# Modulation sections with four column sets side by side and one sum per section; gate rows broadcast by DMA through DRAM

## The chip, the cores and the metric

The kernel runs on one core of one Trainium2 chip. The metric is the device time of one execution in microseconds (us). Inside the core TensorE (PE; its weight loads are PEld), VectorE (DVE), ScalarE (ACT) and GpSimd (POOL) each work through their own instructions in order; SyncE (SP) issues all DMA transfers of this kernel, in order too.

## What is computed

Two layers of an encoder over 256 tokens of width 1024. Each layer has a token mixer (attention, retention and a state space branch S5) and a convolutional feed-forward net (FFN). What matters here is the modulation by the vector c:

```python
cond = jax.nn.silu(c)
for l in range(DEPTH):                       # DEPTH = 2
    mod = cond @ w_ada[l] + b_ada[l]         # (1, 1024) @ (1024, 6144)
    shift1, scale1, gate1, shift2, scale2, gate2 = jnp.split(mod, 6, axis=-1)
    h = layer_norm(x) * (1.0 + scale1) + shift1
    merged = ...                             # the mixer, fed by h @ w_in[l]
    x = post_norm(ALPHA * x + gate1 * (merged @ w_o[l]))
    h = layer_norm(x) * (1.0 + scale2) + shift2
    x = post_norm(ALPHA * x + gate2 * conv_ffn(h))
```

So there are twelve modulation sections of 1024 values, six in a layer, and each is a product of one row with a 1024x1024 matrix. A shift or a scale is needed as a column (the channel lies on the partitions); a gate is needed as a row that stands in all 128 partitions.

## The kernel before, in words

Tokens lie in two tiles of 128 (t = 0 and 1). Weights come from DRAM as loads of 128x1024 floats (512 KB), named `raw` for the main weights and `ada` or `adab` for `w_ada`. The main weights are split into two parts (`hi` by ACT, `lo` by DVE), so that a product takes three matmuls; some products (`g_ps`) use `raw` itself.

**The modulation** is done by `ada_chunk` (L1110). A section is four chunks of 256 columns, a chunk is two loads, and a load holds four row blocks of 128 times 256 columns. Four matmuls with 32-column weights (`condz`, in which only the first of 32 columns is not zero) write the four row blocks' partial sums side by side into partitions 0, 32, 64 and 96 of one PSUM bank, `ada_ps`; the second load adds to them. Then ACT copies the bank to `z`. For a gate, a matmul with a 128x128 matrix of ones (L1126) adds the four partial sums and puts the result into all partitions, and DVE adds the bias row (`rows`, L1128). For a shift or scale, two transposes (L1131) bring `z` to columns, DVE adds the four (L1133) and then the bias.

**The order.** All operations are recorded first. A planner (`Recorder.schedule`, L546) then sets each engine's order, from costs, priorities in recorded order, and free buffers. Six kinds of place matter:
- `need` (L1153) inserts chunks between weight loads of the mixer (`spread`, L1890). The rest (`adab`) are recorded behind the boundaries (L1896, L1908).
- A **boundary** (`boundary`, L1264) follows the mixer and the FFN. For t = 0 and then t = 1, DVE multiplies the result by the gate (`y`), normalizes (`bst`, `bmv`, `ve`, `x`) and prepares the next norm; POOL gives `rstd`. The normalized `xn` is transposed on PE (`h_ps`), modulated by ACT (`hf`), split (`hh`, `hlo`), and feeds the next product (`upt` for the FFN, `b_` for the next mixer).
- Before the first boundary of a layer stand the output product `wo_acc` and, ahead of it, `br_ps`, which waits for `th` and `osl` (DVE) behind `glu_ps`.
- The S5 branch sends a matrix `R` through DRAM (`rd`, L1740) and loads it back as 32 transfers named `T`, which PE needs for `Y`.
- SP issues in the planned order; an issue waits until its tile is free and its source is there.
- `rot` (L1331) makes rotation tables of the next layer on DVE, wherever the planner finds room.

Of the kernel before, what the change touches and what calls it, by code (L numbers as in the profile page):

```python
# [10 lines left out]
F32 = mybir.dt.float32  # L11
# [3 lines left out]
ALU = mybir.AluOpType  # L15
AX = mybir.AxisListType
# [3 lines left out]
D = 1024  # L20
S = 256
P = 128
# [36 lines left out]
SEC = ("shift1", "scale1", "gate1", "shift2", "scale2", "gate2")  # L59


def _rows(w):
    k = w.shape[0] // P
    return w.reshape(k, P, w.shape[1]).transpose(1, 0, 2)
# [82 lines left out]
    return out  # L147


def _ada(w, l, key):  # L150
    c, k = (int(v) for v in key[3:].split("_"))
    return _rows(w["w_ada"][l][k * 512:(k + 1) * 512, c * 256:(c + 1) * 256]).reshape(P, -1)


# [32 lines left out]
def _host(w):  # L187
# [3 lines left out]
    for g in _stream():  # L191
        cols = [(_ada(w, l, key) if fn is None else fn(w, l)).astype(f32, copy=False)
                for l, key, width, fn in g]
        parts.append(np.concatenate(cols, axis=1).ravel())
# [537 lines left out]
def build(tc, A, dbg=None):  # L732
    nc = tc.nc
    ctx = ExitStack()
    rec = Recorder()

    def pool(name, bufs, **kw):
        return Pool(rec, ctx.enter_context(tc.tile_pool(name=name, bufs=1, **kw)), bufs, kw.get("space") == PSUM)

    cp = pool("const", 1)  # L740
    drp = pool("dram", 1, space=DRAM)
# [6 lines left out]
    V, G, T, AC, SY = (Engine(rec, n, e) for n, e in (  # L748
        ("DVE", nc.vector), ("POOL", nc.gpsimd), ("PE", nc.tensor), ("ACT", nc.scalar), ("SP", nc.sync)))
    mm = T.matmul  # L750

    def t4(shape, name, dt=F32):
        return k4.tile(shape, dt, tag="k4", name=name)
# [4 lines left out]
    def t1(shape, name, dt=F32):  # L758
        return k1.tile(shape, dt, tag="k1", name=name)

    def bank(shape, name):
        return psp.tile(shape, F32, tag="ps", name=name)
# [10 lines left out]
    def tt(out, a, b, op, eng=None, flex=False):  # L773

        eng = eng or main[0]
        eng.tensor_tensor(out=out, in0=a, in1=b, op=op, **({"alt": G if eng is V else V} if flex else {}))

    def ts(out, a, s1, op0, s2=None, op1=None, eng=None):
        eng = eng or main[0]
        if eng is G and op1 is None:  # L780
            s2, op1 = 1.0, ALU.mult
        kw = {} if op1 is None else {"op1": op1}
        eng.tensor_scalar(out=out, in0=a, scalar1=s1, scalar2=s2, op0=op0, **kw)

    def stt(out, a, s, op0, b, op1):
        if main[0] is V:
            V.scalar_tensor_tensor(out=out, in0=a, scalar=s, in1=b, op0=op0, op1=op1)
        else:
            tmp = gtmp[:, 0:a.shape[1]]
            ts(tmp, a, s, op0)  # L790
            tt(out, tmp, b, op1)
# [14 lines left out]
    for gi, g in enumerate(groups):  # L806
        offs.append(o)
        c = 0
# [6 lines left out]
    def raw_chunk(l, key, tile_=None):  # L815

        gi, c, width = where[l, key]
        if gi not in loaded:
            w = sum(x[2] for x in groups[gi])
            t = loaded[gi] = tile_ or t4([P, 1024], "raw")  # L820
            SY.dma_start(out=t[:, 0:w], in_=A["wts"][offs[gi]:offs[gi] + P * w].rearrange("(p w) -> p w", p=P))
        return loaded[gi][:, c:c + width]
# [33 lines left out]
    ident = const[:, 0:P]  # L856
    dist = const[:, P:640]

    def sm(name, a=0, b=None):
        lo, hi = off[name]  # L860
        return small[:, lo + a:(hi if b is None else lo + b)]

    ones = cp.tile([P, P], F32, name="ones")
    V.memset(ones, 1.0)
    mhalf = cp.tile([P, 16], F32, name="mhalf")
    gtmp = cp.tile([P, 80], F32, name="gtmp")
    G.memset(mhalf, -0.5)
# [6 lines left out]
    condz = cp.tile([P, 8, 32], F32, name="condz")  # L874
# [223 lines left out]
    modc = {}  # L1098
    gate_rows = {}

    def row_tile(l, i):
        t = t4([P, D], "rows" if i < 2 else "lnrow")
        SY.dma_start(out=t, in_=A["rows"][l, i:i + 1, :].to_broadcast([P, D]))
        return t

    for l in range(L):
        for s in ("shift1", "scale1", "shift2", "scale2"):
            modc[l, s] = cp.tile([P, 8], F32, name=f"mod{l}{s}")

    def ada_chunk(l, c, kind=None):  # L1110
        sec, sub = SEC[c // 4], c % 4
        ps = bank([P, 512], "ada_ps")
        for j in range(2):
            raw = t4([P, 1024], kind or "ada")
            raw = raw_chunk(l, f"ada{c}_{j}", raw).rearrange("p (k n) -> p k n", k=4)
            with rec.group():
                for k in range(4):
                    mm(out=ps[32 * k:32 * k + 32, 0:256], lhsT=condz[:, 4 * j + k], rhs=raw[:, k],
                       start=(j == 0), stop=(j == 1))
        z = t1([P, 256], "z")  # L1120
        AC.copy(z, ps[:, 0:256])
        if sec.startswith("gate"):
            i = 0 if sec == "gate1" else 1
            if sub == 0:
                gate_rows[l, sec] = row_tile(l, i)
            mm(out=ps[:, 256:512], lhsT=ones, rhs=z, start=True, stop=True)  # L1126
            g = gate_rows[l, sec][:, sub * 256:(sub + 1) * 256]
            tt(g, ps[:, 256:512], g, ALU.add)  # L1128
        else:
            for b in range(2):  # L1130
                T.transpose(ps[:, 256 + b * P:256 + (b + 1) * P], z[:, b * P:(b + 1) * P], ident)  # L1131
            m = modc[l, sec][:, 2 * sub:2 * sub + 2]
            V.tensor_reduce(out=m, in_=ps[:, 256:512].rearrange("p (b c d) -> p b c d", b=2, d=32)[:, :, :, 0],  # L1133
                            op=ALU.add, axis=AX.X)
            ib = ("shift1", "scale1", "shift2", "scale2").index(sec)
            bcol = sm("b_ada", l * 32 + ib * 8 + 2 * sub, l * 32 + ib * 8 + 2 * sub + 2)
            if sec.startswith("scale"):
                stt(m, m, 1.0, ALU.add, bcol, ALU.add)
            else:
                tt(m, m, bcol, ALU.add)  # L1140


    pending, pace = [], [0, 1]
# [5 lines left out]
    def settle():  # L1149
        while pending:  # L1150
            ada_chunk(*pending.pop(0))

    def need(l, key):  # L1153
        pace[0] += 1
        if pending and pace[0] > 0 and pace[0] % pace[1] == 0:
            rec.bias = ADA_BIAS
            ada_chunk(*pending.pop(0))
            rec.bias = 0
        return chunk(l, key)
# [222 lines left out]
    def mixer(l, xt, h, s5, xdram, ready=None, pre_=None):  # L1382
# [10 lines left out]
        if h is None:  # L1393
            h, xn = new_h(l, 1), [norm(x) for x in xt]
            for k in range(0, 8, 2):
                for c in (k // 2, 4 + k // 2):
                    ada_chunk(l, c, "ada0")
                for t in range(2):
                    put_h(h, l, 1, t, xn[t], [k, k + 1])
                gemm_t(need(l, f"b0_{k}"), h, 416, k, o0, k == 0, k == 6)  # L1400
                b1(k)
            rope_tables()
            rec.bias = PRE_BIAS
            prephase()
            s5.prep()
            s5.rot()
            rec.bias = 0
        elif ready is not None:
            ps0, ps1 = ready[0:2], ready[2:4]
            o0 = [q[:, 0:416] for q in ps0]  # L1410
# [476 lines left out]
    h, s5, start = None, S5(0), None  # L1887
    for l in range(L):
# [12 lines left out]
        if more:  # L1901
            start = Start(l + 1, FIRST)
# [37 lines left out]
```

## Time and profile before

| | us |
|---|---|
| three runs, median | 1078.13 (1076.7 to 1079.13) |
| the profiled execution, its own time | 1076.2 |
| its span | 1074.3 |
| PE busy | 998.9 (93%) |
| DVE busy | 860.2 (80%) |
| ACT busy | 492.0 (46%) |

The profile names the line of the recording helper (L728) for nearly all instructions, so they are told apart by tile. The stages in the order of time: first norm and modulation (0 to 130), first mixer (130 to 345), first boundary (345 to 375), FFN (to 553), second boundary (553 to 600), second mixer (to 857), its boundary (857 to 890), FFN and last norm. All DMA goes through SP: 212 MB in all.

### The profile page before, as it was taken

Reading aid. Unit: us, or ns where it says so; the run is one execution under the profiler, and the core shown is the slowest. Engines: PE = TensorE matmul, PEld = TensorE weight load, DVE = VectorE, ACT = ScalarE, POOL = GpSimd, SP = SyncE. Lnnn points to the kernel's source line nnn. Section 1 sums busy time; section 2 is a strip of 40 time slices with the busy share of each in tenths; the row PEclk is TensorE's granted clock in tenths of the full one; section 3 lists DMA queues with packets and bytes.
Section 4 is the critical chain, followed back from the end, with each engine's and each line's share of the span. In section 5 each row is a group of like instructions: output and inputs, shape, how many; then the busy total and the mean of one; then the engine's idle time right before and its main releaser. Section 6 shows DMA issues by size and latency. Waiting matters only on the chain.

```text
span 1074.3 us, 20654 instructions
## 1 busy us (share of the span) xinstructions
PE 998.9 (93%) x8148; PEld 852.6 (79%) x8148; DVE 860.2 (80%) x1783; ACT 492.0 (46%) x888; POOL 37.8 (4%) x43
## 2 busy tenths in 40 slices
PE   4878999998999999999989999998699979999996
PEld 2557876776888689999967988777599859999995
DVE  7999999973569998777888997997365698777775
ACT  2353343212563666555635645411256456555640
POOL 0010000000001100000011000000000010000001
PEclk9989999998999999999998999999899989999998
DMA  8963235448874966555559532543877437555510
GB/s 337 408 231 125 92 125 190 155 121 268 326 261 168 377 244 222 190 179 178 169 197 374 187 117 77 219 157 79 259 252 274 138 120 233 187 189 193 200 36 40
DMA packets 66849, 212.09 MB, mean 197 GB/s; under 512 B 7744, under 2 KB 16064, under 8 KB 66752
## 3 DMA queue, kind: packets, MB, share of 16 engines
q1 hardware_dynamic: 66752, 210.77, 56.2%
q8 instruction: 64, 1.05, 0.4%
q14 instruction: 33, 0.27, 0.1%
HBM read 207.66 MB, written 3.08 MB: 196 GB/s over the span
## 4 chain that ended last, share of the span: by engine, by line
PE 66%; DVE 10%; DMA 3%; ACT 1%; issue 1%; POOLq 0%; SPq 0%; DVEq 0%; ACTq 0%
PE up_ps L728 22%; PE dn_acc L728 11%; PE g_ps L728 10%; PE br_ps L728 4%; PE ada_ps L728 3%; PE wo_acc L728 2%; PE upt L728 2%; PE b L728 2%; DVE g L728 2%; DMA ada<-in_wts 1%; DVE w L728 1%; DVE y L728 1%; PE u_ps L728 1%; PE glu_ps L728 1%; DVE x L728 1%
## 5 line engine op out<-in xcount | busy, mean ns | idle before, releaser
L728 DVE TENSOR_TENSOR lo<-raw,hi 128x1024 fp32r<-128x1024 f32 (+1 forms) x210 | 251.3, 1214 | 65.1 <-PE up_ps L728 20.1
L728 ACT CAST hi<-raw 128x1024 fp32r<-128x1024 f32 (+1 forms) x210 | 214.3, 1043 | 73.2 <-DVE lo L728 18.3
L728 PE MATMUL up_ps<-hh,lo 128*128 128x256 f32 x640 | 181.1, 283 | 0.0
L728 PE MATMUL up_ps<-hlo,hi 128*128 128x256 f32 x640 | 181.1, 283 | 0.0
L728 PE MATMUL up_ps<-hh,hi 128*128 128x256 f32 x640 | 181.0, 283 | 0.0
L728 PE MATMUL g_ps<-hw,raw 128*128 128x256 f32 x512 | 124.8, 387 | 0.0
L728 PEld LDWEIGHTS up_ps<-hh,hi 128*128 128x128 f32 x640 | 122.7, 192 | 1.7 <-DVE g L728 0.4
L728 PEld LDWEIGHTS up_ps<-hlo,hi 128*128 128x128 f32 x640 | 122.7, 192 | 1.2
L728 PEld LDWEIGHTS up_ps<-hh,lo 128*128 128x128 f32 x640 | 122.7, 192 | 0.1
L728 PEld LDWEIGHTS g_ps<-hw,raw 128*128 128x128 f32 x512 | 94.2, 192 | 16.8 <-issue 5.8
L728 DVE SCALAR_TENSOR_TENSOR cv<-up_ps,small,cv 128x255 f32<-128x255 f32 x176 | 73.2, 475 | 13.0 <-ACT cv L728 12.8
L728 PE MATMUL dn_acc<-lo,ah 128*128 128x512 f32 x176 | 68.7, 391 | 0.0
L728 PE MATMUL dn_acc<-hi,al 128*128 128x512 f32 x176 | 67.1, 390 | 0.0
L728 PE MATMUL dn_acc<-hi,ah 128*128 128x512 f32 x176 | 66.8, 392 | 0.0
L728 ACT ACTIVATE cv<-up_ps,small 128x256 f32<-128x256 f32 x88 | 44.9, 562 | 33.4 <-PE up_ps L728 33.0
L728 ACT ACTIVATE gt<-g_ps 128x256 f32<-128x256 f32 x48 | 18.4, 384 | 86.2 <-PE g_ps L728 86.1
L728 ACT CAST hl<-raw 128x512 fp32r<-128x512 f32 x48 | 28.9, 619 | 42.6 <-DMA raw<-in_wts 19.1
L728 DVE TENSOR_TENSOR hl<-raw,hl 128x512 fp32r<-128x512 f32 x48 | 32.5, 685 | 16.4 <-ACT hl L728 16.1
L728 DVE TENSOR_TENSOR w<-g,g 128x512 f32<-128x512 f32 x64 | 42.9, 685 | 0.7 <-PE br_ps L728 0.5
L728 POOL TENSOR_TENSOR rstd<-ve,mhalf 128x1 f32<-128x1 f32 (+1 forms) x28 | 30.0, 1077 | 347.7 <-DVE ve L728 347.7
L728 DVE TENSOR_TENSOR g<-bC,pw 128x512 f32<-128x512 f32 x64 | 41.7, 682 | 0.1
L728 DVE TENSOR_TENSOR g<-pw,bbt 128x512 f32<-128x512 f32 x64 | 41.0, 684 | 0.0
(324 smaller groups left out, 2149.6 us busy)
## 6 DMA issues: line engine op xcount, KB each, us to landing
raw<-in_wts SPq DMA_DIRECT2D x262, 512.0 KB, 4.4
ada<-in_wts SPq DMA_DIRECT2D x48, 512.0 KB, 9.5
adab<-in_wts SPq DMA_DIRECT2D x48, 512.0 KB, 7.0
T<-rd SPq DMA_DIRECT2D x64, 64.0 KB, 3.1
lnrow<-in_rows SPq DMA_DIRECT2D x8, 512.0 KB, 5.2
raw<-in_wts SPq DMA_DIRECT2D x8, 416.0 KB, 6.9
x<-in_x SPq DMA_DIRECT2D x4, 512.0 KB, 7.2
rows<-in_rows SPq DMA_DIRECT2D x4, 512.0 KB, 6.5
```

Source lines behind the costliest of these rows:

```text
L728: getattr(o.eng.real, method)(*a, **kw)
```

## The change

The sections shift1 and scale1 of layer 0 stay as they were. For the other ten, `ada_part` replaces the sum by chunk:
- A load now holds one row block of 128 with all 1024 columns of the section. Its four matmuls share the weights of that row block, and their outputs side by side are four sets of 256 columns instead of four partial sums. All eight loads of a section add to the same bank.
- After the last load, and only then, one copy to `z` and, for shift and scale, two transposes and one addition with the bias.
- For a gate, the four rows of `z` are written to DRAM by four DMAs (`zd`, 1 KB each), one DMA reads them back into all 128 partitions (512 KB, `rows<-zd`), and one DVE addition of 128x1024 adds the bias row, which is loaded as before. The matrix of ones is gone.

```diff
+def ada_rows(l, c):
+    return (l, c // 4) not in ((0, 0), (0, 1))
 def _ada(w, l, key):
     c, k = (int(v) for v in key[3:].split("_"))
+    if ada_rows(l, c):
+        k += 2 * (c % 4)
+        return w["w_ada"][l][k * P:(k + 1) * P, c // 4 * D:(c // 4 + 1) * D]
...
-    ones = cp.tile([P, P], F32, name="ones")
-    V.memset(ones, 1.0)
...
+    def ada_part(l, c, kind):
+        sec, sub = SEC[c // 4], c % 4
+        if sub == 0:
+            ada_bank[l, sec] = bank([P, 512], "ada_ps")
+        ps = ada_bank[l, sec]
+        for j in range(2):
+            raw = t4([P, 1024], kind or "ada")
+            raw = raw_chunk(l, f"ada{c}_{j}", raw)
+            with rec.group():
+                for q in range(4):
+                    mm(out=ps[32 * q:32 * q + 32, 0:256], lhsT=condz[:, 2 * sub + j], rhs=raw[:, q * 256:(q + 1) * 256],
+                       start=(sub + j == 0), stop=(sub == 3 and j == 1))
+        if sub < 3:
+            return
+        z = t1([P, 256], "z")
+        AC.copy(z, ps[:, 0:256])
+        if sec.startswith("gate"):
+            i = 0 if sec == "gate1" else 1
+            brow, g = row_tile(l, i), t4([P, D], "rows")
+            zd = drp.tile([1, D], F32, name=f"zd{l}{i}")
+            for q in range(4):
+                SY.dma_start(out=zd[:, q * 256:(q + 1) * 256], in_=z[32 * q:32 * q + 1])
+            SY.dma_start(out=g, in_=zd.to_broadcast([P, D]))
+            tt(g, g, brow, ALU.add)
+            gate_rows[l, sec] = g
+        else:
+            for b in range(2):
+                T.transpose(ps[:, 256 + b * P:256 + (b + 1) * P], z[:, b * P:(b + 1) * P], ident)
+            v = ps[:, 256:512].rearrange("p (b s d) -> p s b d", b=2, d=32)[:, :, :, 0]
...
+            if sec.startswith("scale"):
+                stt(m, v, 1.0, ALU.add, bcol, ALU.add)
+            else:
+                tt(m, v, bcol, ALU.add)
...
     def ada_chunk(l, c, kind=None):
+        if ada_rows(l, c):
+            return ada_part(l, c, kind)
...
-            mm(out=ps[:, 256:512], lhsT=ones, rhs=z, start=True, stop=True)
-            g = gate_rows[l, sec][:, sub * 256:(sub + 1) * 256]
-            tt(g, ps[:, 256:512], g, ALU.add)
```

The planner orders the whole program anew. Three places show what that does; a row is an instruction, with its count where it repeats, `condz` marks the modulation matmuls and four of them belong to one load.

PE in the first boundary of layer 0, from the end of `wo_acc` to the start of `upt`, before:

```order
L728 MATMUL wo_acc<-hi,ml 128x512
L728 MATMUL ada_ps<-z,ones 128x256
L728 MATMUL ada_ps<-adab,condz 32x256 x16
L728 MATMUL ada_ps<-z,ones 128x256
L728 MATMUL ada_ps<-adab,condz 32x256 x12
L728 MATMUL h_ps<-const,xn 128x128 x8
L728 MATMUL ada_ps<-z,ones 128x256
L728 MATMUL ada_ps<-const,z 128x128 x2
L728 MATMUL ada_ps<-adab,condz 32x256 x8
L728 MATMUL upt<-hi,hh 128x512
```

and after the change:

```order
L736 MATMUL wo_acc<-hi,ml 128x512
L736 MATMUL ada_ps<-adab,condz 32x256 x32
L736 MATMUL h_ps<-const,xn 128x128 x8
L736 MATMUL upt<-hi,hh 128x512
L736 MATMUL upt<-lo,hh 128x512
```

The products with ones are gone, the transposes of `z` come much later, and eight loads stand together ahead of `h_ps`.

DVE in the first mixer, ahead of and behind the two `th`, before:

```order
L728 SCALAR_TENSOR_TENSOR th<-th,zF 128x512
L728 SCALAR_TENSOR_TENSOR osl<-th,osh 128x512
L728 SCALAR_TENSOR_TENSOR th<-th,zF 128x512
L728 TENSOR_TENSOR lo<-raw,hi 128x1024
L728 SCALAR_TENSOR_TENSOR osl<-th,osh 128x512
```

and after the change, two rows more at the start:

```order
L736 TENSOR_TENSOR lo<-raw,hi 128x1024
L736 TENSOR_TENSOR rows<-rows 128x1024
L736 SCALAR_TENSOR_TENSOR th<-th,zF 128x512
L736 SCALAR_TENSOR_TENSOR osl<-th,osh 128x512
L736 SCALAR_TENSOR_TENSOR th<-th,zF 128x512
```

The addition of the broadcast gate1 row (`rows<-rows`) now stands directly ahead of the first `th`.

DVE in the first boundary of layer 1, the part of t = 1, before:

```order
L728 TENSOR_TENSOR y<-y,xa 128x512
L728 TENSOR_TENSOR rows<-ada_ps,rows 128x256
L728 BN_STATS bst<-y 128x6
L728 TENSOR_TENSOR rows<-ada_ps,rows 128x256
L728 BN_AGGR bmv<-bst 128x2
L728 TENSOR_TENSOR rows<-ada_ps,rows 128x256
L728 TENSOR_SCALAR ve<-bmv 128x1
L728 SCALAR_TENSOR_TENSOR x<-y,bmv,lnrow 128x1024
L728 TENSOR_TENSOR lo<-raw,hi 128x1024
L728 TENSOR_TENSOR hlo<-hf,hh 128x4x128
```

and the later part of the same stretch after the change, up to `xn`:

```order
L736 SCALAR_TENSOR_TENSOR x<-y,bmv,lnrow 128x1024
L736 TENSOR_TENSOR hlo<-hf,hh 128x4x128
L736 SCALAR_TENSOR_TENSOR x<-x,rstd,lnrow 128x1024
L736 TENSOR_TENSOR hlo<-hf,hh 128x4x128
L736 BN_STATS bst<-x 128x6 x2
L736 BN_AGGR bmv<-bst 128x2
L736 TENSOR_SCALAR ve<-bmv 128x1
L736 TENSOR_TENSOR rows<-rows 128x1024
L736 TENSOR_TENSOR lo<-raw,hi 128x1024
L736 TENSOR_SCALAR xn<-x,bmv,rstd 128x1024
```

The three additions of 256 columns and one `lo` are gone from this stretch, and the addition of the whole gate2 row stands ahead of `xn`. What SP issues for it, after the change:

```order
L736 DMA raw<-in_wts 128x1024 x5
L736 DMA lnrow<-in_rows 128x1024
L736 DMA rows<-in_rows 128x1024
L736 DMA raw<-in_wts 128x1024 x13
L736 DMA zd_9563<-z 1x256 x4
L736 DMA rows<-zd_9563 128x1024
L736 DMA raw<-in_wts 128x1024 x48
```

where before there stood:

```order
L728 DMA x<-xs_6478 128x1024
L728 DMA raw<-in_wts 128x1024 x5
L728 DMA lnrow<-in_rows 128x1024
L728 DMA raw<-in_wts 128x1024 x3
L728 DMA rows<-in_rows 128x1024
L728 DMA raw<-in_wts 128x1024 x62
```

Four small writes and the read back now stand between the weight loads of the FFN.

## Rows read from the trace of the kernel before

**Rows 1.** Stretches: us, busy of PE, PEld, DVE, ACT, POOL (x), PEclk, DMA share, GB/s.

```profile
130.00:242.00 112.00, 109.08 (x1224) 82.48 (x1223) 100.36 (x221) 34.10 (x94) 2.64 (x2) 1.00 0.44 142
260.00:345.00 85.00, 85.00 (x617) 74.76 (x614) 60.94 (x90) 45.79 (x71) 1.36 (x3) 1.00 0.75 277
360.30:390.00 29.70, 29.70 (x234) 22.59 (x235) 28.24 (x73) 20.47 (x40) 1.51 (x1) 1.00 0.85 329
571.00:600.00 29.00, 29.00 (x207) 24.55 (x206) 25.17 (x71) 14.46 (x35) 3.62 (x5) 1.00 0.93 369
680.00:745.00 65.00, 60.67 (x823) 47.93 (x821) 61.41 (x140) 19.36 (x55) 2.64 (x2) 1.00 0.41 134
765.00:857.00 92.00, 91.40 (x654) 81.69 (x647) 56.26 (x83) 46.78 (x72) 0.00 (x0) 0.99 0.68 237
862.00:873.00 11.00, 4.55 (x29) 2.91 (x22) 10.89 (x21) 4.92 (x11) 3.57 (x3) 0.71 0.42 136
```

**Rows 2.** The chain that ended last: start us, us, what (xcount).

```profile
242.22 8.21 DMA ada<-in_wts
...
752.78 7.00 DMA ada<-in_wts
```

**Rows 3.** Tile ada_ps: groups with ns min/median/max, first and last start.

```profile
L728 PE MATMUL ada_ps<-const,z x64: 270/272/476, 17.6 to 596.8; 128*128 128x128 f32 x64
L728 PE MATMUL ada_ps<-z,ones x32: 377/379/483, 263.0 to 863.7; 128*128 128x256 f32 x32
```

**Rows 4.** The chain again, at a product with ones and at a pair of transposes.

```profile
263.21 0.43 PE ada_ps L728 x2
...
381.42 0.22 PE ada_ps L728 x2
```

**Rows 5.** The timeline (start us, us, instruction xcount), first boundary of layer 0.

```profile
347.88 0.19 DVE L728 TENSOR_TENSOR g<-rot,rot 128x32 f32<-128x32 f32 x1
347.99 0.21 DVE L728 BATCH_NORM_AGGREGATE bmv<-bst 128x2 f32<-128x12 f32 x1
351.73 1.93 PE L728 MATMUL ada_ps<-adab,condz 128*32 128x256 f32 x32
```

**Rows 6.** The timeline of DVE in the first boundary of layer 1, t = 1.

```profile
868.69 0.42 DVE L728 TENSOR_TENSOR rows<-ada_ps,rows 128x256 f32<-128x256 f32 x1
869.03 0.68 DVE L728 BATCH_NORM_STATS2 bst<-y 128x6 f32<-128x512 f32 x1
...
876.70 0.15 DVE L728 TENSOR_SCALAR ve<-bmv 128x1 f32<-128x1 f32 x1
876.77 2.35 DVE L728 TENSOR_TENSOR lo<-raw,hi 128x1024 fp32r<-128x1024 f32 x2
```

**Rows 7.** The timeline of SP's issues (303, 860 to 870), and of DVE at 312.99.

```profile
303.43 0.33 SPq L728 DMA_DIRECT2D raw<-in_wts  x1
...
312.99 0.68 DVE L728 SCALAR_TENSOR_TENSOR th<-th,zF 128x512 f32<-128x512 f32 x1
...
860.33 2.88 SPq L728 DMA_DIRECT2D raw<-in_wts  x2
868.80 0.33 SPq L728 DMA_DIRECT2D raw<-in_wts  x1
```

**Rows 8.** DMA issues (KB each, median us to landing); tile rows: landing of `rows<-in_rows`; tile rd.

```profile
rd<-R SPq DMA_DIRECT2D x16, 60.0 KB, 2.1
...
DMA to landing us min/median/max: 3.4/6.5/8.3
...
DMA to landing us min/median/max: 1.9/2.9/7.9
```

**Rows 9.** PE: timeline at 868.91, and the chain's two first halves of upt.

```profile
868.91 1.97 PE L728 MATMUL h_ps<-const,xn 128*128 128x128 f32 x8 [4.84 <-ACT xn L728]
...
360.93 5.72 PE upt L728 x24
872.48 7.88 PE upt L728 x24
```

More of the change, by code (lines that the diff above doesn't have):

```diff
@@ L1108, in build @@
             modc[l, s] = cp.tile([P, 8], F32, name=f"mod{l}{s}")
+    ada_bank = {}
+    def ada_part(l, c, kind):
[27 more added lines that the diff above has]
+            v = ps[:, 256:512].rearrange("p (b s d) -> p s b d", b=2, d=32)[:, :, :, 0]
+            m = modc[l, sec].rearrange("p (s b) -> p s b", b=2)
+            ib = ("shift1", "scale1", "shift2", "scale2").index(sec)
+            bcol = sm("b_ada", l * 32 + ib * 8, l * 32 + ib * 8 + 8).rearrange("p (s b) -> p s b", b=2)
+            if sec.startswith("scale"):
+                stt(m, v, 1.0, ALU.add, bcol, ALU.add)
+            else:
+                tt(m, v, bcol, ALU.add)
     def ada_chunk(l, c, kind=None):
+        if ada_rows(l, c):
+            return ada_part(l, c, kind)
         sec, sub = SEC[c // 4], c % 4
@@ L1121, in ada_chunk @@
         AC.copy(z, ps[:, 0:256])
[L1122 to L1125, printed above, removed]
-            mm(out=ps[:, 256:512], lhsT=ones, rhs=z, start=True, stop=True)
-            g = gate_rows[l, sec][:, sub * 256:(sub + 1) * 256]
-            tt(g, ps[:, 256:512], g, ALU.add)
-        else:
[L1130 to L1140, printed above, removed]
+        for b in range(2):
+            T.transpose(ps[:, 256 + b * P:256 + (b + 1) * P], z[:, b * P:(b + 1) * P], ident)
+        m = modc[l, sec][:, 2 * sub:2 * sub + 2]
+        V.tensor_reduce(out=m, in_=ps[:, 256:512].rearrange("p (b c d) -> p b c d", b=2, d=32)[:, :, :, 0],
+                        op=ALU.add, axis=AX.X)
+        ib = ("shift1", "scale1", "shift2", "scale2").index(sec)
+        bcol = sm("b_ada", l * 32 + ib * 8 + 2 * sub, l * 32 + ib * 8 + 2 * sub + 2)
+        if sec.startswith("scale"):
+            stt(m, m, 1.0, ALU.add, bcol, ALU.add)
+        else:
+            tt(m, m, bcol, ALU.add)
     pending, pace = [], [0, 1]
```

## The prediction

> **What bounds the kernel now.** I read the stretches first, then the chain that ended last, then the timelines at its bends. The stretches [rows 1] show stages with different limits. From 260 to 345 us, from 360.3 to 390 and from 571 to 600 PE is busy for the whole stretch, from 765 to 857 for 91.4 of 92 us: there a PE instruction taken away shortens the time by its own step. From 680 to 745 DVE (61.4 of 65) is the bound, from 130 to 242 both are nearly full (PE 109, DVE 100 of 112). In the first boundary of layer 1 (862 to 873) DVE is full (10.9 of 11) and PE works 4.6 us: there only DVE's chain counts. At 242 and 753 PE stands and waits for transfers, 8.2 and 7.0 us of the chain [rows 2]: PE work taken away just ahead of those two places is worth nothing.
>
> **The change part by part.** *Kept:* 96 loads, each with four 32-column matmuls; only the layout in DRAM and the place of the sums differ. A load costs PE 1.93 / 4 = 0.48 us (32 records are two passes of 16 matmuls, so four loads) [rows 5]. *Removed from PE:* 16 products with ones, in the trace 32 records, and 36 of 64 transposes (ten sections: six columns sections go from 8 to 2) [rows 3]. Their durations of 379 and 272 ns are latencies; what they take of PE's time is the chain's step: 0.43 us for a product with ones and 0.22 for a pair of transposes [rows 4]. In all that is 16 x 0.43 + 18 x 0.22 = 10.8 us, the most that PE can give back. By stage, counting in the two orders what stands inside the full stretches:
>
> - First mixer after its stall (260 to 345): five ones go, 2.15 us; one load more stands there, since a boundary gives it up, 0.48. Gain 1.67.
> - First boundary of layer 0, from 360.3: five pairs and one load go, 1.10 + 0.48. In DVE's chain ahead of it the planner now sets five small rot operations between `bst` and `x` of t = 0; one costs a step of 0.11 us [rows 5], together 0.5 against. Gain 1.1. The three ones at the start of that boundary fall into PE's wait for DVE and give nothing.
> - Second boundary, from 571: four pairs, 0.9.
> - First mixer, 130 to 242: three pairs, 0.66, with DVE spared as many reductions and small additions; since two engines share the bound there, 0.6.
> - Second mixer: the ones ahead of the stall at 753 are hidden by it. Behind it three ones go, 1.29, and two loads come, 0.96: 0.33. From 680 to 745 DVE loses one addition of 256 columns, whose step is 0.34 (868.69 to 869.03) [rows 6]: 0.3.
> - First boundary of layer 1: three such additions leave the chain of t = 1, 3 x 0.34 = 1.0. PE's three ones there lie in its idle time: nothing.
>
> That sums to 1.67 + 1.1 + 0.9 + 0.6 + 0.33 + 0.3 + 1.0 = 5.9 us.
>
> *ACT* loses 30 copies; it is nowhere the bound, so nothing. *PSUM:* a bank is now held for a whole section instead of a chunk. The orders show the same matmuls in nearly the same places through both mixers, so I take nothing; if a bank were short, the products behind it would have moved.
>
> *Added:* 16 writes of 1 KB, four broadcast reads of 512 KB (2 MB beside 212), and four DVE additions of 128x1024. The nearest row for an addition is `lo` of the same size, 1.2 us [rows 6]; four of them replace 16 steps of 0.34, so DVE's sum is about level. The new wait is the way through DRAM. The trace has a copy of it: `rd<-R` lands 2.1 us after issue in the median, the S5 tile's transfers take 1.9 to 7.9, and a row broadcast to 128 partitions takes 3.4, 6.5 or 8.3 (least, median, most) [rows 8]. Three of the four gates have time:
> - gate2 of layer 0 is needed only at the second boundary, and its addition stands behind the last `hlo` of the first one; no row tells when it lands there, so its cost has the bounds 0 and the 3.0 of the case below, and I take 0.
> - gate1 of layer 1: its addition stands among `lo` operations that run ahead of need.
> - gate2 of layer 1: its writes follow 13 loads, the last of which is issued at 860.3 to 863.2; four issues of about 0.4 (a load's takes 0.33) [rows 7] end at 864.8, the writes land by 866.9, the read is issued by 867.3 and lands at 873.8 in the median. DVE gets there at `ve` (876.70) less the 1.0 saved and the `lo` of 1.2 (two in 2.35) that has left [rows 6]: 874.5. Just in time; behind it waits `xn`. SP itself waits there for `z` and then for the writes, with 48 loads of the FFN behind it; today its next load goes out only at 868.80 [rows 7], so 867.3 delays none.
>
> The fourth, gate1 of layer 0, is tight: its writes follow a load issued at 303.43 [rows 7], one load comes between, so the read is issued at about 306.7 and lands at 313.2 in the median. DVE reaches it at about 312, since `th` stood at 312.99 and the addition takes the place of one `lo`. Behind it wait `th`, `osl`, and with them `br_ps` on PE. I charge 0.7 us; the bounds are 0 (landing in 3.4) and 3.0 (in 8.3).
>
> So the gain is 5.9 - 0.7 = 5.2 us. The profiled execution took 1076.2 us, 1.9 below the median of the runs; the same difference from the median gives 1078.1 - 5.2 = 1072.9.
>
> **The rivals.** *The DVE queue stops at the broadcast.* DVE works in order, so a late row holds up everything behind the addition, in two places on the path. If each transfer takes the longest of its rows, the first mixer loses 3.0 us; in layer 1 the writes land at 864.8 + 7.9, the read 0.4 later plus 8.3, at 881.4, against 874.5: 6.9 lost. Together 10 against a gain of 5.9: 4 us slower, 1082. It turns the sign once the two waits sum to more than 5.9, and most likely through the second, since the first cannot. Against it: from 862 to 873 the DMA engines are busy for 0.42 of the time, so landings should be near the median or better [rows 1].
>
> *The clock falls in one boundary more.* In the first boundary of layer 1 PE idles 4.84 us before `h_ps`, and the clock falls there: the granted clock of 862 to 873 is 0.71, 2.4 GHz for part and 1.2 for the rest [rows 1, 9]. With it the first half of `upt` takes 7.88 us where the same 24 matmuls took 5.72 at the full clock in layer 0: 2.2 us [rows 9]. The first boundary of layer 0 keeps its clock now because modulation work fills PE's wait; the change takes three ones and some transposes out of exactly that filling. If the clock falls there too, 2.2 of the 5.2 us go: 1075.1. The Trainium skill, "TensorE: Matmul & The Clock Gate", section "HAM oscillation — how this bites in real kernels", says that a gap in which PE idles lets the clock fall to half, so that the work behind it starts slow; by that rule the time would be 1075.1, and the trace agrees in layer 1. For the forecast speaks that eight loads, 3.9 us of PE, now stand together in that wait (seven before).
>
> *The bound is elsewhere.* The new order moves many rows by a few places. If the full stretches of PE are full because of work that can wait (prefetched splits, gates), the instructions taken out leave gaps instead of time, as at the two stalls. Then only the DVE terms stay, 1.0 + 0.3 less 0.7: 1077.5, no change.
>
> **How the numbers follow.** Forecast (gain of 2.9 to 10.8 us): 0.54. Clock: 0.13. Bound elsewhere: 0.16. DVE stop: 0.17, with a loss of 0 to 4 us and more. A difference under 0.2%, 2.2 us, cannot be told from no change. The forecast and the clock case (3.0 us of gain) are faster: 0.67. Bound elsewhere is the same: 0.16. The stop is slower: 0.17. The range starts at 1066, where all of PE's 10.8 us and the 1.3 of DVE come back, and goes to 1081, nearly the full stop; what lies outside is about 0.05 below and 0.12 above.
>
> **What would show it.** In the profile of the changed kernel PE's busy time should be lower by about 10 us and the ones gone; DVE's wait at `rows<-rows` ahead of `th` should be under 2 us and at most small ahead of `xn` in layer 1; the time from the first stall's end to the first `y` should shrink by about 1 us, and the two waits for `T` should stay at 8 and 7. The granted clock of the first boundary of layer 0 should stay 1.00. It is wrong if DVE idles at `rows<-rows` for more than 3 us, if new idle time of PE appears in the mixers (a PSUM bank or a transfer that comes late), or if the waits for `T` change by more than 2 us, as the writes and reads of the gates share SP with them.

## The result, and the profile after

The changed kernel takes 1064.36 us in the median of four runs (1062.51 to 1066.9), the kernel before 1078.63 beside it. The ratio is 0.9871, with a 95% interval of 0.9844 to 0.9899: 13.9 us less, 10.9 to 16.8. The forecast was 1072.9 with a range of 1066 to 1081: the sign was right, the gain is 2.7 times the 5.2 us of the sum. The profiled execution of after took 1065.51 us (span 1063.7), that of before 1076.2 (span 1074.3).

The page of after, its busy times and the shares of the chain that ended last:

```profile
PE 991.2 (93%) x8080; PEld 848.8 (80%) x8080; DVE 855.2 (80%) x1729; ACT 480.3 (45%) x857; POOL 31.6 (3%) x43
...
PE 77%; DVE 14%; DMA 5%; issue 1%; ACT 1%; SPq 0%; POOL 0%; POOLq 0%; DVEq 0%; ACTq 0%
```

PE's busy time fell by 7.7 us (998.9 before), less than the 10.8 of the sum of removed work, and PE is still busy for 93% of the span, with 77% of the chain. So the saved PE work alone cannot be the 13.9 us.

The stretches that answer to [rows 1] (the same columns; the borders lie at other places in the work, so the lengths of two stretches must not be compared):

```profile
130.00:245.50 115.50, 112.03 (x1234) 85.41 (x1233) 101.50 (x220) 34.46 (x96) 2.34 (x2) 0.99 0.42 137
264.00:348.50 84.50, 84.50 (x630) 73.33 (x623) 60.03 (x87) 43.72 (x66) 1.17 (x3) 0.99 0.79 293
361.90:391.50 29.60, 29.08 (x220) 22.08 (x221) 29.01 (x59) 18.07 (x35) 0.88 (x2) 1.00 0.87 339
571.00:600.00 29.00, 29.00 (x207) 24.45 (x206) 26.96 (x66) 14.95 (x35) 3.36 (x5) 1.00 0.93 370
680.00:741.80 61.80, 57.19 (x769) 46.15 (x770) 58.64 (x134) 16.57 (x48) 2.35 (x2) 1.00 0.43 142
768.60:855.30 86.70, 86.70 (x627) 76.60 (x616) 63.70 (x89) 48.23 (x72) 1.85 (x2) 1.00 0.74 264
855.30:862.60 7.30, 3.30 (x26) 1.98 (x24) 6.77 (x14) 4.87 (x10) 1.86 (x2) 0.75 0.32 87
```

The mixers up to their stalls and the full stretches have kept their limits. Two places have shrunk by more than their saved work, measured between the same instructions: the second mixer behind its stall (from the first `Y` that waits for `T` to the start of the last `wo_acc`, 95.9 us before and 92.2 after), and the first boundary of layer 1 (from there to the first `upt`, 12.35 and 7.38).

**Stage by stage.** The table takes the start of the first or last matmul of a kind as the border of each stage, and shows by how much each stage became shorter (-) or longer: by the prediction, in the two profiled executions, and in the run with only the PE work left out (below).

| stage (layer) | predicted | after - before | PE work left out - before |
|---|---|---|---|
| start to last `kps` (0) | -0.6 | +3.5 | +0.8 |
| to last `wo_acc` (0) | -1.67 + 0.7 | -0.1 | -2.2 |
| to first `dn_acc` (0), the boundary in it | -1.1 | -2.3 | -0.6 |
| to first `u_ps` (1), FFN and second boundary | -0.9 | -1.1 | -0.1 |
| to last `kps` (1) | -0.3 | -1.8 | +0.1 |
| to last `wo_acc` (1), the stall in it | -0.33 | -3.0 | -1.6 |
| to first `upt` (1), the boundary | -1.0 | -5.0 | 0.0 |
| to the end | 0 | -0.8 | -0.1 |
| sum | -5.2 | -10.65 | -3.7 |

The sum is the difference of two single executions, 1076.2 and 1065.51; the 3.2 us that are missing to the 13.9 of all runs stand in no stage.

**The first boundary of layer 1: -5.0.** DVE before (timeline: start us, us, instruction; in brackets idle time ahead and what ended it):

```profile
856.93 1.29 DVE L728 TENSOR_TENSOR y<-wo_acc,rows 128x512 f32<-128x512 f32 x2 [8.00 <-PE wo_acc L728]
...
861.49 1.28 DVE L728 SCALAR_TENSOR_TENSOR x<-y,bmv,lnrow 128x1024 f32<-128x1024 f32 x1
```

PE before, at the product that ends just ahead of `y` (856.51 + 0.39 = 856.90):

```profile
856.51 0.39 PE L728 MATMUL wo_acc<-lo,mh 128*128 128x512 f32 x1
```

And DVE after:

```profile
845.67 0.69 DVE L736 TENSOR_TENSOR y<-wo_acc,rows 128x512 f32<-128x512 f32 x1
847.51 0.69 DVE L736 TENSOR_TENSOR y<-wo_acc,rows 128x512 f32<-128x512 f32 x1 [1.15 <-PE wo_acc L736]
...
852.04 1.28 DVE L736 SCALAR_TENSOR_TENSOR x<-y,bmv,lnrow 128x1024 f32<-128x1024 f32 x1 [1.49 <-PE wo_acc L736]
```

In both traces `wo_acc` of t = 0 is complete well before the products of t = 1 end. Before, DVE stands for 8.00 us all the same, and starts both halves of `y` together at 856.93, 3.2 us before the last product (860.13). After, the halves start at 845.67 and 847.51, each when its own sum is there, and only `x` waits, 1.49 us. The wait before was not one for data. In the planner's assignment `y` of t = 0 stands before in a place of the 4 KB pool that a `lo` of `wo_acc` leaves late, and after in one that an earlier `raw` has left; PE's reading of that `lo` is what DVE waited for (the run y_apart below shows it). PE waits 2.4 us for `xn` after, 4.84 before [rows 9], and the first half of `upt`, 7.88 us there, takes 7.22:

```profile
859.05 1.13 PE h_ps L736 x4
...
862.62 7.22 PE upt L736 x24
```

**The stall of the second mixer: -3.0.** PE's timeline before, at the products ahead of `Y<-T` and at the wait:

```profile
753.69 2.42 PE L728 MATMUL g_ps<-hw,raw 128*128 128x256 f32 x10
764.24 1.08 PE L728 MATMUL Y<-T,U 128*32 128x128 f32 x16 [8.13 <-DMA T<-rd]
```

And after:

```profile
751.79 3.72 PE L736 MATMUL g_ps<-hw,raw 128*128 128x256 f32 x16
...
757.01 0.40 PE L736 MATMUL br_ps<-orh,hl 128*128 128x256 f32 x2
763.04 1.08 PE L736 MATMUL Y<-T,U 128*32 128x128 f32 x16 [5.62 <-DMA T<-rd]
```

`T` comes at about the same time, 764.24 and 763.04, or 20.5 and 21.2 us behind the start of the last `kps`. But PE has ten matmuls of `g_ps` to do in the wait before, and sixteen and a group of `br_ps` after: the wait is 2.5 us shorter, and what was done in it is not left for later. No run took this apart from the rest of the new order.

**The way through DRAM: no wait of DVE.** SP's issues of gate1 of layer 0, and DVE at the addition there and at that of gate2 of layer 1:

```profile
305.01 1.17 SPq L736 DMA_DIRECT2D zd<-z  x4
...
309.60 0.34 SPq L736 DMA_DIRECT2D rows<-zd  x1
```

```profile
314.68 1.22 DVE L736 TENSOR_TENSOR rows<-rows 128x1024 f32<-128x1024 f32 x1
316.08 0.69 DVE L736 SCALAR_TENSOR_TENSOR th<-th,zF 128x512 f32<-128x512 f32 x1 [0.17 <-ACT th L736]
...
866.63 1.21 DVE L736 TENSOR_TENSOR rows<-rows 128x1024 f32<-128x1024 f32 x1
```

No bracket stands at either addition: DVE did not idle ahead of them. The read was issued at 309.60, later than the 306.7 that I had worked out, but DVE came only at 314.68. SP, in contrast, stood 7.3 us for `z` ahead of the writes of gate2 of layer 1, with weight loads behind it; PE's waits of that boundary are for `xn` and `hh`, not for a load.

### The profile page after: what moved, and what is told of

It is laid out like the page before. It is cut to its first block, busy times and chain, and to the rows that moved or that the text cites. A ratio compares the mean times of both kernels' runs of the same rounds, so it can differ in the third digit from the quotient of the medians.

```text
span 1063.7 us, 20435 instructions
## 1 busy us (share of the span) xinstructions
PE 991.2 (93%) x8080; PEld 848.8 (80%) x8080; DVE 855.2 (80%) x1729; ACT 480.3 (45%) x857; POOL 31.6 (3%) x43
## 4 chain that ended last, share of the span: by engine, by line
PE 77%; DVE 14%; DMA 5%; issue 1%; ACT 1%; SPq 0%; POOL 0%; POOLq 0%; DVEq 0%; ACTq 0%
PE up_ps L736 22%; PE g_ps L736 13%; PE dn_acc L736 11%; PE br_ps L736 5%; PE b L736 5%; PE wo_acc L736 4%; DMA ada<-in_wts 3%; DVE g L736 2%; PE ada_ps L736 2%; PE upt L736 2%; DMA adab<-in_wts 1%; PE w_ps L736 1%; DVE lo L736 1%; PE St L736 1%; DVE arena L736 1%
## 5 line engine op out<-in xcount | busy, mean ns | idle before, releaser
L736 DVE SCALAR_TENSOR_TENSOR cv<-up_ps,small,cv 128x255 f32<-128x255 f32 x176 | 73.2, 476 | 14.9 <-ACT cv L736 14.7
L736 PEld LDWEIGHTS dn_acc<-hi,al 128*128 128x128 f32 x176 | 33.0, 188 | 7.3
```

What stands on the lines that cost most here:

```text
L736: getattr(o.eng.real, method)(*a, **kw)
```

## The experiments

The gain in us is (1 - ratio) x 1078.6, with the ratio's interval. "Boundary" is the time from the start of the last `wo_acc` to that of the first `upt` in layer 1, "y waits" DVE's longest wait for `wo_acc` ahead of a `y` of t = 0 there, "T waits" PE's longest wait for `T` in the second mixer; these three are from each run's profiled execution. The kernels with "work_out" compute other gate rows and other modulation sections than the reference.

| kernel | median us | gain us (95%) | boundary | y waits | T waits |
|---|---|---|---|---|---|
| before | 1078.63 | | 12.35 | 8.0 | 8.1 |
| after | 1064.36 | 13.9 (10.9 to 16.8) | 7.38 | 1.1 | 5.6 |
| y_apart | 1076.16 | 2.6 (0.9 to 4.4) | 8.70 | 2.0 | 8.3 |
| x_apart | 1064.81 | 13.6 (11.1 to 16.2) | 6.13 | 1.4 | 6.6 |
| columns_only | 1071.63 | 6.9 (4.4 to 9.5) | 11.63 | 8.0 | 2.4 |
| gates_only | 1072.37 | 6.1 (3.8 to 8.6) | 6.57 | 1.2 | 7.5 |
| before_seed1 | 1077.47 | 1.9 (-0.3 to 4.1) | 11.99 | 8.0 | 6.1 |
| before_seed2 | 1080.19 | -1.9 (-3.6 to -0.3) | 11.99 | 8.0 | 5.6 |
| before_seed3 | 1085.90 | -8.3 (-11.2 to -5.5) | 12.00 | 7.5 | 7.5 |
| before_seed4 | 1072.03 | 5.5 (2.7 to 8.4) | 6.64 | none | 2.4 |
| after_seed1 | 1076.23 | 3.0 (1.2 to 5.0) | 12.03 | 7.4 | 5.3 |
| after_seed2 | 1073.51 | 5.8 (3.8 to 7.8) | 12.00 | 7.6 | 5.4 |
| after_seed3 | 1068.04 | 10.5 (6.8 to 14.0) | 6.58 | 1.2 | 5.7 |
| after_seed4 | 1065.38 | 12.3 (9.7 to 14.9) | 6.66 | 1.2 | 6.4 |
| pe_work_out | 1076.03 | 4.0 (2.3 to 5.8) | 12.34 | 8.0 | 7.7 |
| pe_work_out_y | 1072.27 | 7.8 (5.8 to 9.8) | 9.16 | 2.0 | 8.8 |
| rows_early | 1065.27 | 15.1 (12.5 to 17.7) | 6.57 | 1.2 | 5.4 |
| after_y_x_planned | 1063.90 | 15.5 (13.3 to 17.8) | 5.82 | 1.4 | 5.8 |

### One tile in a place of its own

After the planning, so that no order changes, `y` is put into a table of the S5 branch that is dead by then:

```diff
+            own[l, i, t] = y, x1
     rec.plan()
+    own[1, 1, 0][0].tile = bbt.real()[:, 0:1024]
```

> The kernel before, every engine's order word for word the same; only the tile y of t = 0 in the first boundary of layer 1 gets a place of its own (the S5 table that nobody reads any more there) instead of one of the 37 places of 4 KB, in which the last w_o operand stood. Theory 'place' (in the kernel before, the first y waits for its place until the last w_o product, 856.93 us, though its sum is done some 9 us earlier; in the changed kernel it got an earlier free place): the y steps run beside the w_o products, only x still waits for the last product, and the time from the last w_o product to xn falls from 12.0 us to about 7.3; the gain is 4.6 us, to 6.8 if PE's wait gets so short that the clock stays up: 1072 to 1074. Theory of the prediction (the gain is PE work taken out of full stretches): no change, 1078.6 within 1.

Measured: 2.6 us less (0.9 to 4.4); the boundary became 3.65 shorter. DVE there:

```profile
850.04 0.69 DVE L728 TENSOR_TENSOR bbt<-wo_acc,rows 128x512 f32<-128x512 f32 x1 [0.74 <-PE wo_acc L728]
852.76 0.69 DVE L728 TENSOR_TENSOR bbt<-wo_acc,rows 128x512 f32<-128x512 f32 x1 [2.03 <-PE wo_acc L728]
...
858.65 1.28 DVE L728 SCALAR_TENSOR_TENSOR x<-bbt,bmv,lnrow 128x1024 f32<-128x1024 f32 x1 [2.85 <-PE wo_acc L728]
```

The mechanism is shown: with nothing but the place changed, the 8.0 us go and each half starts when its sum is done. The size was not 4.6, because the next wait stands behind it: `x` has its own place from a still later w_o operand, which it gets at 858.65, where before it started at 861.49. A gain of nothing is excluded by the interval, though its lower end, 0.9, just reaches the "within 1" of that expectation.

In the changed kernel `x` is moved as well:

```diff
+    own[1, 1, 0][0].tile = bbt.real()[:, 0:1024]
+    own[1, 1, 0][1].tile = pw.real().rearrange("p a b c -> p (a b c)")[:, 0:1024]
```

> The changed kernel, every engine's order the same; y and x of t = 0 in the first boundary of layer 1 get places of their own (two S5 tables that are no longer read there). Theory 'place': x no longer waits 1.5 us (852.04) for the last w_o product; 1.5 us less, to 3.0 if the clock then stays up in that boundary: 1061.4 to 1062.9. Theory of the prediction: DVE's chain there counts as well, but nothing in it says that x waits for a place, so no change, 1064.4.

Measured: the same as after (13.6 against 13.9), with intervals of some 2.5 us to either side, so neither expectation is excluded by the time. `x` no longer waits, and the boundary is 1.25 shorter, as expected; PE then waits 2.02 instead of 1.6 us ahead of `upt`, whose stage takes 16.97 us instead of 16.05, so most is given back:

```profile
860.95 1.09 PE L736 MATMUL h_ps<-const,xn 128*128 128x128 f32 x8 [1.63 <-ACT xn L736]
864.06 0.80 PE L736 MATMUL upt<-hi,hh 128*128 128x512 f32 x1 [2.02 <-ACT hh L736]
```

### The two halves of the change

In the first, the new way is limited to the shift and scale sections, in the second to the gates:

```diff
-    return (l, c // 4) not in ((0, 0), (0, 1))
+    return (l, c // 4) not in ((0, 0), (0, 1)) and not SEC[c // 4].startswith("gate")
```

```diff
-    return (l, c // 4) not in ((0, 0), (0, 1))
+    return SEC[c // 4].startswith("gate")
```

> Only the shift and scale sections are worked off four column sets side by side; the gate sections stay as before, with their products with ones. By the prediction's terms: pairs of transposes out of full stretches, 1.1 in the first boundary of layer 0, 0.9 in the second, 0.6 in the first mixer: 2.6 us less, 1076. Theory 'order' (the list planner draws a new order and new places at every edit, and what that is worth is larger than the work saved): the two halves do not add up to the whole; this one between 1070 and 1082, without relation to 2.6.

> Only the gate sections are worked off in the new way, with the rows broadcast by DMA through DRAM; shift and scale sections stay as before. By the prediction's terms: five and three products with ones out of full stretches and the row additions, 2.15 + 1.29 + 0.3 + 1.0 less loads and charge: some 3 us less, 1075.5. Theory 'order': between 1070 and 1082, and with the other half not adding up to the whole gain of 14 us.

Measured: 6.9 and 6.1, in sum 13.1 against 13.9. Both are over twice the prediction's terms, and against the expectation of "order" they add up. But the profiled executions show that neither is mainly its own work: the columns gain 5.3 us between the last `kps` and the first `glu_ps` of layer 1, where PE's wait for `T` fell from 8.1 to 2.4, and nothing of `y`'s wait; the gates gain 5.8 in the boundary, where `y`'s wait went, and the wait for `T` stays at 7.5. Two different gains of the order sum to about the whole, in which each is present in part; nothing here shows that they had to.

### Other orders of the same two kernels

The planner adds small random shifts to the priorities. Another seed gives the same instructions in another order and other places:

```diff
-JITTER = (17, 2)
+JITTER = (1, 2)
```

> The kernel before with another seed of the planner's small random shifts of priority (1 instead of 17): the same instructions and tiles, another order and other places. With seeds 1 to 4 of both kernels this prices the order alone. Theory 'order': the seeds of one kernel lie 4 us or more apart, and 17 happens to be good for the changed kernel; the mean gain over the seeds is then near the 5.2 of the prediction. Theory 'place and filling': the gain of 14 us holds in the mean over the seeds too (10 to 14), because the change leaves more places of 4 KB free and lets PE's waits be filled. For this kernel: 1076 to 1086, and the first y of layer 1's first boundary starts at the end of the w_o products, as with seed 17.

> The kernel before with seed 2, otherwise as the run with seed 1. Both theories: 1076 to 1086; the y of t = 0 in layer 1's first boundary in a place that the last w_o operand leaves.

> The kernel before with seed 3. As with seed 1: theory 'order' has the seeds of one kernel 4 us or more apart and a mean gain of the change near 5; theory 'place and filling' a mean gain of 10 to 14. For this one 1076 to 1090.

> The kernel before with seed 4: here the y of t = 0 in layer 1's first boundary gets a place that an earlier raw tile leaves, as the changed kernel with seed 17. Theory 'place': DVE's wait of 8 us ahead of the first y is gone and the time lies 3 to 5 us under the other seeds of this kernel. Without the place being the cause: no relation to it.

> The changed kernel with seed 1. Its y of t = 0 in layer 1's first boundary stands in a place that a w_o operand leaves, as in the kernel before, while seed 17 gave it one that an earlier raw tile leaves. Theory 'place': it loses some 4 to 5 us there against seed 17, 1069 to 1071, and DVE waits several us for the w_o products ahead of y. Theory of the prediction (work taken out): within 2 us of 1064.4.

> The changed kernel with seed 2; y of t = 0 again in a place that a w_o operand leaves. Theory 'place': 1069 to 1071. Theory of the prediction: within 2 us of 1064.4. Over the seeds, theory 'order': a mean gain near 5; theory 'place and filling': 10 to 14.

> The changed kernel with seed 3; y of t = 0 in layer 1's first boundary in a place that a raw tile leaves, as with seed 17. Theory 'place': the time from the last w_o product to xn is about 7 us as with seed 17; 1064 to 1070. For the mean over the seeds as with the others.

> The changed kernel with seed 4; y of t = 0 again in a place that a raw tile leaves. Theory 'place': 1064 to 1070, about 7 us from the last w_o product to xn. For the mean over the seeds: 'order' a gain near 5, 'place and filling' 10 to 14.

Measured: the five orders of the kernel before lie between 5.5 us of gain and 8.3 of loss, the five of the changed kernel between 3.0 and 13.9 of gain. The mean ratios are 1.0005 and 0.9916: in the mean the change gives 9.7 us, with a standard error of 3.1 from the spread of the seeds. That excludes neither the 5.2 of the sum nor the 14 of seed 17, which is the best of the five for the changed kernel, 4.8 us better than their mean, and is near the mean for the kernel before. Two expectations failed: after_seed1 and after_seed2 were put at 1069 to 1071 from the late place alone and took 1076.23 and 1073.51, so their orders lose elsewhere too.

What the seeds do show is the place. The boundary takes 11.6 to 12.4 us in all runs in which `y` stands in a late place, and 5.8 to 7.4 in all with an early one (8.7 and 9.2 with `x` still late), in both kernels. One row of after_seed1 and two of before_seed4:

```profile
855.87 1.29 DVE L736 TENSOR_TENSOR y<-wo_acc,rows 128x512 f32<-128x512 f32 x2 [7.43 <-PE wo_acc L736]
```

```profile
847.89 0.69 DVE L728 TENSOR_TENSOR y<-wo_acc,rows 128x512 f32<-128x512 f32 x1
850.79 0.69 DVE L728 TENSOR_TENSOR y<-wo_acc,rows 128x512 f32<-128x512 f32 x1
```

So the changed kernel can have the long wait (seeds 1 and 2), and the kernel before can be without it (seed 4, which is 5.5 us faster than seed 17 and also has PE's wait for `T` down to 2.4). Between kernels with the same kind of place, the mean ratios are 1.0019 and 0.9959 (late), 0.9949 and 0.9887 (early): 6.5 and 6.7 us for the change. With one to four orders in each group this is a hint and not a measurement, but it lies near the sum of 5.2.

### The saved work alone

The order of the kernel before is planned as it was; then the 16 products with ones and 36 transposes are taken out of the list:

```diff
     rec.plan()
+    for o, new in drop.items():
+        o.calls = [(m, a, {**kw, new[0]: new[1]}) for m, a, kw in o.calls] if new else []
```

> The kernel before with its order and its places kept as they are; only the PE instructions that the change saves are left out: the 16 products with ones and 36 of the transposes (18 pairs, in the six sections that the change converts). The additions and reductions that read their results read the bank's products instead and stay in place, so the gate rows and six of the eight modulation sections are not the reference's. Theory of the prediction (work inside full stretches of PE is time): five ones 2.15, five pairs 1.10, four pairs 0.9, three pairs 0.66, three ones 1.29 = 6.1 us less than before; no DVE term, since the additions stay. Theory 'bound elsewhere': 0 to 2 us less. Theory 'order': whatever this gives, the rest of the 14 us is order and places, some 8 us.

> As the run with the PE work left out (gate rows and six modulation sections are not the reference's), and the y of t = 0 in layer 1's first boundary in a place of its own as well. If work and place simply add: the gain of the first plus 2.6 (the whole run y_apart against before) to 3.7 (its boundary alone). By the prediction's work term and the place: 6.1 + 2.6 to 3.7 = 8.7 to 9.8 less than before. If both only make PE wait longer elsewhere: less than 6.

Measured: 4.0 us (2.3 to 5.8), and with `y` apart 7.8 (5.8 to 9.8). The saved PE work is worth 4.0, under the 6.1 of the terms; the place adds 3.8, so work and place add within their intervals. In this run the additions read the bank's products and no longer wait for `z` and the product with ones, so the 4.0 holds that saved wait too, which the change keeps in another form. Some 6 us of the 13.9 (2.5 to 9.7 by the two intervals) are then neither. The place of `x` is part of them: the boundary of after is 1.8 us shorter than that of pe_work_out_y (7.38 against 9.16). The rest is put down to the order (the shorter wait for `T`, the boundary of layer 0) and to the saved DVE and ACT steps only because it is left over; no run took it apart. The stage table shows where the work counted: -2.2 behind the first stall and -1.6 in the second mixer. From the first to the second boundary it was worth 0.7 of 2.0. In the second boundary the wait of the loads ended up longer (PE's waits from 540 to 620 us, before and with the work left out: us in all, times, the longest):

```profile
PE ada_ps L728 <- DMA adab<-in_wts: 2.7, 3, 1.5
```

```profile
PE ada_ps L728 <- DMA adab<-in_wts: 3.3, 3, 2.5
```

### Why the place comes early, and whether more can be had

The only tile whose life the change shortens for sure is the gate's bias row, loaded now with the section's last chunk. It is loaded with the first again:

```diff
         if sub == 0:
             ada_bank[l, sec] = bank([P, 512], "ada_ps")
+            if sec.startswith("gate"):
+                gate_rows[l, sec] = row_tile(l, 0 if sec == "gate1" else 1)
```

> The changed kernel, but a gate's bias row is loaded with the section's first chunk, as in the kernel before, and so holds a place of 4 KB for the whole section. If the shorter hold of that row is what frees the early place for y: the wait of y for the w_o products comes back and 3 to 5 us are lost, 1067 to 1069. If it is not: 1064.4 within 1.5, and y starts beside the w_o products as in the changed kernel.

Measured: the same as after (15.1 against 13.9), and `y` starts as early. A loss of 3 to 5 us from 13.9 lies outside the interval. So the early place does not need the row's shorter hold. Last, `y` and `x` of t = 0 have their own places already when the order is planned:

```diff
+            if (l, i, t) == (1, 1, 0):
+                y, x1 = bbt[:, 0:D], pw.rearrange("p a b c -> p (a b c)")[:, 0:D]
+            else:
+                y, x1 = t4([P, D], "y"), t4([P, D], "x")
```

> The changed kernel with y and x of t = 0 in layer 1's first boundary in two S5 tables that nobody reads any more, this time known to the planner, which may use the two places of 4 KB for other tiles. Theory 'place': the 1.5 us of x's wait go and the order may follow it: 1061.5 to 1063.5. If the next limit there is PE itself and the transfers: 1064.4 within 1.5.

Measured: 1063.9, a gain of 15.5 (13.3 to 17.8), which cannot be told from after, so neither expectation is excluded. The boundary has its shortest time, 5.82 us.

## Why the prediction was wrong, point by point

- **The step that failed is "First boundary of layer 1: there only DVE's chain counts", sized at 1.0.** I read that chain from its middle, at t = 1 [rows 6], and took away three row additions. They were not in the chain that ends at `h_ps`: they stand at 868.69 and later, and ACT had begun `xn` of t = 0 at 867.62 (the row below, before). Ahead of the chain stood DVE's 8.00 us for `y`, to which the prediction gives no term: the stretch from which it read the limit, 862 to 873 [rows 1], starts behind it. The boundary gained 5.0; y_apart shows that the wait is one for a place, and that the place alone shortens the boundary by 3.65.

```profile
867.62 1.24 ACT L728 ACTIVATE xn<-x,nmr,rstd 128x1024 f32<-128x1024 f32 x1 [4.30 <-DVE nmr L728]
```

- **"The two waits for T should stay at 8 and 7"** failed. The 8 and 7 were pieces of the chain that belong to loads of `ada` [rows 2]; PE's own waits for `T` were 5.0 and 8.1 before, and 6.3 and 5.6 after. The prediction takes PE work ahead of such a wait as worth nothing. I did not ask whether the new order would put more work into the wait; in the second mixer it did, and that stage gained 3.0 instead of 0.33.
- **PE's work in full stretches**: the mechanism held, the size was 4.0 (2.3 to 5.8) for terms of 6.1. "Five ones go, 2.15" came out in the stage with the work alone (2.2). In the changed kernel the first mixer behind its stall is 2.3 us shorter as well (97.6 and 95.4 from `Y` to the last `wo_acc`, for 1.67), but `T` came 2.1 later behind the last `kps` (20.25 and 22.38), and the stage gained 0.1. The terms of the two layer-0 boundaries, 1.1 and 0.9, measured 0.6 and 0.1 with the work alone, in single executions. PE's busy time fell by 7.7, and by 7.5 with the work alone, not by "about 10": the 10.8 were too much.
- **First mixer, 0.6**: not seen. That stage became 3.5 us longer in the profiled pair. In y_apart, whose order is that of before, it is 1.5 longer too, so part is a difference between executions (see the last section). The prediction named new idle time of PE as a sign of being wrong, and ahead of the mixer there is some: PE waits 5.1 us for `uT` at 95.9, a wait that the trace of before does not have. It is not the change's alone, since seeds 1 to 3 of the kernel before have it too (3.1, 4.6 and 2.2):

```profile
PE U_ps L736 <- DVE uT L736: 5.1, 1, 5.1
```

- **The charge of 0.7** for the gate row ahead of `th` measured 0, the lower bound, and gate2 of layer 1 needed none either. The working had a gap: it issues the read at 306.7, 1.0 us behind the last write's issue (305.7), where the writes alone take 2.1 to land. Worked out as for layer 1, the read is issued at 308.2 and its row is 2.7 us late against DVE's 312. That nothing was lost is luck by that working: DVE came later than thought, at 314.68. The rival of the stopped DVE queue is out.
- **The clock in the boundary of layer 0** stayed at 1.00 (354.3 to 361.9 us), as forecast, although PE waits up to 2.1 us there. In the boundary of layer 1 it still falls (0.75 from 855.3 to 862.6), with waits of 2.4 and 1.6 us. The Trainium skill, "TensorE: Matmul & The Clock Gate", section "HAM oscillation — how this bites in real kernels", says that a gap in which PE idles lets the clock fall. The rows of layer 1 agree; those of layer 0 show a gap that did not.
- **ACT and PSUM nothing**: no row speaks against it, and no run tests it. "The bound is elsewhere" (no change) is out.
- **The range** left out gains over 12 us, since it took PE's whole saved work and DVE's steps as the most there is. A change that makes the planner draw a new order has no such end: the orders of one kernel alone lie 13.8 us apart.

What stays open: why the gates' new way gives `y` an early place with seeds 17, 3 and 4, and the old way only with seed 4. The shorter hold of the bias row is not needed for it. What the remaining 6 us consist of is open too. Five orders each are too few to say that the change makes it likelier.

## What to carry to other kernels

Where a planner sets the order and the buffers, an edit is two changes, the work and a new drawing; price the work by taking it out of the old order, and run both kernels with several drawings before the difference is put down to the edit. A wait that the profile puts down to an engine whose result was done long before can be, as here, a wait for a buffer: ask what stood in the tile's place, and try the tile in a place of its own. At a stall that ends with a transfer, count the work that the order puts into it, and not only the work ahead that is saved.

## What was unexpected in the hardware

Executions of the same program differ by some 6 us: rows_early took 1060.97 to 1067.26, y_apart 1073.26 to 1078.73. Two stretches of rows_early (the execution of 1060.97) and of after (us, busy times, then granted clock):

```profile
0.00:60.00 60.00, 40.24 (x289) 25.75 (x290) 53.12 (x247) 21.44 (x45) 3.60 (x12) 1.00 0.97 377
...
240.00:275.00 35.00, 30.65 (x222) 24.64 (x221) 16.16 (x25) 10.64 (x18) 0.00 (x0) 0.95 0.82 256
```

```profile
0.00:60.00 60.00, 41.51 (x279) 27.08 (x280) 50.87 (x238) 19.60 (x44) 2.72 (x10) 0.91 0.96 377
...
240.00:275.00 35.00, 28.71 (x211) 23.29 (x210) 10.89 (x18) 7.32 (x15) 0.00 (x0) 0.85 0.76 244
```

PE waits in both stretches of both, and the granted clock was higher in the one than in the other (1.00 and 0.95 against 0.91 and 0.85). These are two orders, so the rows alone do not show what one order does from execution to execution; but among the four executions of rows_early the fastest, this one, has the highest mean granted clock (0.983; the others 0.973, 0.968 and 0.972). The stage from the start to the last `kps` took 234.2 us in rows_early and 236.6 in after, the next one to `glu_ps` 72.7 and 75.4. So stages of two single executions are not comparable to better than some 3 us where the clock falls; the stage of 5.0 us in layer 1 stands because all runs with a late place (11.6 to 12.4 us) and all with an early one (5.8 to 7.4, with `x` still late 8.7 and 9.2) agree on it.
